# Latent attention: query tiles split into plain and turned parts, unpadded

## Chip, cores and metric

One core of a Trainium2 chip runs the whole program. The metric is the device time of one execution in microseconds; lower is better. The five engines are TensorE (PE, with weight loads shown apart as PEld), VectorE (DVE), ScalarE (ACT), GpSimd (POOL) and SyncE (SP, which issues most of the transfers here).

## What is computed

Three transformer blocks in a row over 256 tokens of width 1024, in float32: a gated mixer with a feed-forward layer, a differential attention with a convolutional feed-forward layer, and a latent attention with a second such layer. The change lies in the latent attention alone. Its 16 heads have a plain query part of 64 values and a turned (rotary) part of 32; the turned part of the keys is one for all heads. Cut to that:

```python
def mla_attention(h, w_in, q_norm_g, kv_norm_g, w_uq, w_ukv, w_o, cos, sin):
    proj = h @ w_in
    c_q = rms_norm(proj[..., :384], q_norm_g)
    c_kv = rms_norm(proj[..., 384:640], kv_norm_g)
    k_pe = apply_rope(proj[..., 640:], cos, sin)
    q = (c_q @ w_uq).reshape(b, s, 16, 64 + 32)
    q_nope, q_pe = q[..., :64], apply_rope(q[..., 64:], cos, sin)
    kv = (c_kv @ w_ukv).reshape(b, s, 16, 64 + 64)
    k_nope, v = kv[..., :64], kv[..., 64:]
    # for each block of 128 queries
    sc = (einsum('bqhd,bkhd->bhqk', q_nope, k_nope)
          + einsum('bqhr,bkr->bhqk', q_pe, k_pe)) * 96 ** -0.5
    p = masked_softmax(sc, mask)
    o = einsum('bhqk,bkhe->bqhe', p, v)
    return o.reshape(b, s, 1024) @ w_o
```

## The kernel before

Activations lie with their features on the partitions and the 256 tokens along the free dimension. Almost every product of a weight is made three times in float32r, from the high and low halves of weight and activation (`mm3`), each of 128x128 weights and 256 columns. A weight comes by a transfer on SP's queue into one of six `raw` buffers (`load_to`), and is split into its halves three parts ahead of its use: ScalarE copies the high half (line 178), VectorE subtracts the low one (line 179).

`mla` (from line 973) records its work as steps. First come the two latent groups and their norms, the keys (`w_k`, in two halves of the heads) and the values (`v_group`). A pair `p` of heads is then treated in five kinds of steps:

- `q_group(p)`, line 1060: one column group of two 128-row tiles, one for each head of the pair, three k-tiles deep, so 18 products. A head's 96 query rows are padded with zeros to 128: plain part, turned part and zeros, in another order for the second head. `q_evac` (line 1064) turns the whole tile by `rope` (lines 852 to 862): a shuffle, two products with tables and a sum on VectorE and GpSimd.
- `scores(p)`, line 1104: for each head, one product for queries 0 with keys 0 and one for queries 1 with all keys, over 128 rows in plain float32 (lines 1110, 1111); then mask, maxima, one small product, exponentials with their sums on ScalarE (line 1121), reciprocal (line 1124) and division (line 1126). The keys lie padded likewise in two arrays, `ke` and `ko`, into which ScalarE copies the plain parts (line 1079) and spreads the turned part (line 1054).
- `trans(p)`, line 1129: three transposes for each head on TensorE (line 1134), a copy by ScalarE.
- `values(p)`, line 1140: eight recorded passes in two column halves of the array.
- `rows`: 24 products of the output weight's part `p`.

From line 1164 on a round `p` = 3 to 9 holds `q_group(p)`, `trans(p - 2)`, `scores(p - 1)`, the output rows of `p - 4` and `values(p - 2)`. Scores, transposes, values and query groups share four PSUM banks (`at_bank`); query tiles, probabilities and their transposes share ten SBUF buffers (tag `t2`).

Steps are recorded in this order, but the framework that makes the program places each engine's instructions in its own fixed order: by the order of the steps, except that an instruction it expects not to be ready is passed by a later one. In the trace output rows stand ahead of transposes, for instance, and scores between two transposes. On the chip each engine then keeps to that order and waits where something isn't there.

The first attention (`diff_attention`, from line 636) has heads of 64 rows; its score products (lines 721, 722) read either half of the partitions.

Of the kernel before, what the change touches and what calls it, by code (L numbers as in the profile page):

```python
# [16 lines left out]
P = 128  # L17
# [34 lines left out]
def _tables():  # L52
# [7 lines left out]
    ml = np.zeros((P, 2, 2, T), np.float32)  # L60
    ml[:, 0] = 1.0
    kp = np.zeros((P, 2, T), np.float32)
    for slot, o in ((0, 64), (1, 32)):
        ml[o:o + 16, 0, slot], ml[o + 16:o + 32, 0, slot] = c16, c16
        ml[o:o + 16, 1, slot], ml[o + 16:o + 32, 1, slot] = -s16, s16
# [3 lines left out]
    return da, ml, kp  # L69


class Unit:
    """A part of a weight on chip: its two float32r halves, made when it is near its use."""
# [11 lines left out]
class Builder:  # L85
# [114 lines left out]
    def cols(self, banks, u, n, kk, stride, xh, xl, first, last, tiles=None):  # L200
        """Adds one k-tile's products to column tiles; two tiles share a bank."""
# [5 lines left out]
    def group(self, units, banks, ncol, xh, xl, nk=KD, between=None, bank=None):  # L207
        """Steps of one column group, k outermost. banks: list filled at the first step."""
# [90 lines left out]
    def mean_sq(self, ss, n):  # L299
        """Mean of squares + EPS by token, [128, 2]."""  # L300
# [16 lines left out]
    def bcast(self, d, tag="rbc"):  # L317
        """r by token along the free dimension, on all partitions: [128, 256]."""
# [15 lines left out]
    def halves(self, src, hi, lo, eng=None):  # L334
        """Exact float32r halves of an SBUF value."""
# [36 lines left out]
        # what is loaded before the raw part of that number  # L372
# [13 lines left out]
    def stats(self, out, n=D, ss=None):  # L386
        """Two steps: the first gives r by token, the second r along the free dimension."""
# [8 lines left out]
    def token_group(self, units, banks, nk, xh, xl, first=None, between=None):  # L396
        """A 512-wide product with tokens on partitions: two banks, one for each token block."""
# [18 lines left out]
    def mixer(self):  # L416
# [9 lines left out]
        # v: tokens on partitions  # L426
# [31 lines left out]
        # u  # L458
# [12 lines left out]
        # spatial gating, two groups at a time  # L471
# [23 lines left out]
        # cg * xs and its convolution  # L495
# [36 lines left out]
        # gates and the two projections, 512 columns at a time  # L532
# [47 lines left out]
    def conv(self, y, z, name, k, n, bias):  # L580
        """Causal convolution of three taps along the free dimension of one tile."""
# [55 lines left out]
    def diff_attention(self):  # L637
# [6 lines left out]
        def one():  # L644
# [15 lines left out]
            # lambda  # L660
# [49 lines left out]
        def scores(n):  # L710
            # one head; columns: queries 0 with keys 0, queries 1 with keys 0 and 1
# [23 lines left out]
            # p0 / sum0 - lam * p1 / sum1 = (p0 - lam * sum0 / sum1 * p1) / sum0  # L735
# [23 lines left out]
        def values(p):  # L759
            # aT columns: queries 0 with keys 0, queries 1 with keys 0, queries 1 with keys 1  # L760
# [15 lines left out]
            # the rows are still to be divided by sum0  # L776
# [197 lines left out]
    def mla(self):  # L974
# [89 lines left out]
        def q_evac(p):  # L1064
            q[p] = self.rope(qb[p][0], self.ml_c, self.ml_s, swap)
# [244 lines left out]
```

## Time and profile before

| | us |
|---|---|
| median of three runs | 1028.51 |
| lowest, highest | 1023.44, 1029.25 |
| profiled execution, first to last instruction | 1028.4 |
| TensorE busy in it | 1004.9 (98%) |
| VectorE busy in it | 747.3 (73%) |
| ScalarE busy in it | 569.6 (55%) |
| GpSimd busy in it | 174.8 (17%) |

The latent attention, up to the last product of its output rows, lies at about 735 to 830 us of the span. A busy time counts durations from an instruction's start to its end; products overlap each other in TensorE, so the distance between starts tells what one costs there. A product in plain float32 is recorded as two passes. "128\*128" or "64\*128" in a row are the rows and columns of the array in use. A bracket at a row's end is the engine's idle time ahead of it and what ended it.

### The profile page before, as it was taken

The numbers are of one execution on the slowest core, as the hardware profiler recorded it, in microseconds if no ns is written. First come the engines' busy times: TensorE is split into PE (matmuls) and PEld (weight loads), VectorE is DVE, ScalarE is ACT, GpSimd is POOL, SyncE is SP. The second block draws the span as 40 slices with busy tenths as digits, with TensorE's granted clock in tenths as the row PEclk, the third lists the DMA queues.
The fourth block names the chain that finished last, engine by engine and source line by source line (L and its number), as shares of the span: only waits on it lengthen the run. The fifth ranks groups of instructions, "written<-read, shape, count | busy, mean of one in ns | idle before, by whom it ended". The sixth has DMA issues, their size and how long they took to land.

```text
span 1028.4 us, 19647 instructions
## 1 busy us (share of the span) xinstructions
PE 1004.9 (98%) x7934; PEld 967.1 (94%) x7934; DVE 747.3 (73%) x1124; ACT 569.6 (55%) x895; POOL 174.8 (17%) x121
## 2 busy tenths in 40 slices
PE   8999999999999999989899999999998999999997
PEld 6999999999999999988799999999997999999995
DVE  5767766567655655778867977777889988877774
ACT  5744454545444444736665765555686667555552
POOL 3001300002311211451202211010421121101001
PEclk9999999999999999999999999999999999999998
DMA  8764555555555555354245465555453435655531
GB/s 322 240 244 170 184 184 185 188 189 171 192 185 185 184 185 188 116 202 134 101 158 185 157 219 178 191 184 156 157 181 126 145 123 192 203 197 186 184 103 41
DMA packets 50923, 180.36 MB, mean 175 GB/s; under 512 B 5648, under 2 KB 5904, under 8 KB 50832
## 3 DMA queue, kind: packets, MB, share of 16 engines
q1 hardware_dynamic: 50544, 178.58, 51.3%
q8 instruction: 62, 1.02, 0.4%
q10 hardware_dynamic: 288, 0.52, 0.1%
q14 instruction: 29, 0.24, 0.1%
HBM read 178.04 MB, written 1.05 MB: 174 GB/s over the span
## 4 chain that ended last, share of the span: by engine, by line
PE 87%; DVE 4%; ACT 3%; POOL 2%; issue 2%; DMA 1%; SPq 0%; POOLq 0%; DVEq 0%; ACTq 0%
PE mm L193 59%; PE at L193 24%; DVE lo L179 1%; DVE t L862 1%; ACT hi L178 1%; POOL tiny L308 1%; POOL xg L689 1%; DMA xg<-in_xg 1%; PE at L1111 1%; PE at L1134 1%; POOL t L861 1%; ACT b L733 0%; ACT t L1121 0%; PE at L481 0%; ACT b L265 0%
## 5 line engine op out<-in xcount | busy, mean ns | idle before, releaser
L193 PE MATMUL mm<-b,hi 128*128 128x256 f32 x3584 | 642.3, 281 | 1.1 <-DVE b L1023 0.8
L193 PEld LDWEIGHTS mm<-b,hi 128*128 128x128 f32 x3584 | 549.3, 188 | 5.0 <-issue 2.1
L179 DVE TENSOR_TENSOR lo<-raw,hi 128x1024 fp32r<-128x1024 f32 (+2 forms) x336 | 415.9, 1250 | 185.5 <-ACT hi L178 184.6
L178 ACT CAST hi<-raw 128x1024 fp32r<-128x1024 f32 (+2 forms) x337 | 345.4, 1036 | 307.7 <-PE mm L193 237.2
L193 PE MATMUL mm<-b,lo 128*128 128x256 f32 x1792 | 501.1, 280 | 0.0
L193 PEld LDWEIGHTS mm<-b,lo 128*128 128x128 f32 x1792 | 336.9, 188 | 0.7 <-issue 0.7
L193 PE MATMUL at<-b,hi 128*128 128x256 f32 x1088 | 194.3, 280 | 1.0 <-POOL b L337 1.0
L193 PEld LDWEIGHTS at<-b,hi 128*128 128x128 f32 x1088 | 166.3, 188 | 2.2 <-POOL b L337 1.2
L193 PE MATMUL at<-b,lo 128*128 128x256 f32 x544 | 152.0, 279 | 0.0
L193 PEld LDWEIGHTS at<-b,lo 128*128 128x128 f32 x544 | 102.0, 188 | 0.0
L886 POOL TENSOR_TENSOR t<-t,t 128x512 f32<-128x512 f32 x22 | 40.4, 1835 | 289.6 <-DVE t L589 251.1
L589 DVE SCALAR_TENSOR_TENSOR t<-t,par,t 128x254 f32<-128x254 f32 (+1 forms) x176 | 76.1, 486 | 11.6 <-ACT t L587 11.0
L280 POOL TENSOR_TENSOR t<-t,t 128x512 f32<-128x512 f32 x18 | 25.5, 1417 | 190.2 <-ACT t L279 189.7
L193 PE MATMUL at<-hi,b 128*128 128x512 f32 x176 | 56.7, 394 | 0.0
L336 ACT CAST b<-t 128x512 fp32r<-128x512 f32 x50 | 30.9, 621 | 42.1 <-POOL t L886 36.2
L331 DVE TENSOR_TENSOR t<-mm,rbc 128x512 f32<-128x512 f32 x76 | 51.6, 687 | 0.2
L193 PE MATMUL mm<-hi,b 128*128 128x512 f32 x144 | 49.7, 418 | 1.4 <-ACT hi L178 1.4
L337 POOL TENSOR_TENSOR b<-t,b 128x512 fp32r<-128x512 f32 x16 | 29.7, 1864 | 124.7 <-ACT b L336 124.7
L587 ACT ACTIVATE t<-t,par 128x256 f32<-128x256 f32 x88 | 46.0, 591 | 6.4 <-DVE t L331 6.4
L337 DVE TENSOR_TENSOR b<-t,b 128x512 fp32r<-128x512 f32 x34 | 24.3, 719 | 22.8 <-ACT b L336 22.8
L193 PEld LDWEIGHTS at<-hi,b 128*128 128x128 f32 x176 | 32.9, 187 | 7.7
L193 PEld LDWEIGHTS mm<-hi,b 128*128 128x128 f32 x144 | 28.5, 199 | 8.5 <-ACT hi L178 2.1
(181 smaller groups left out, 710.0 us busy)
## 6 DMA issues: line engine op xcount, KB each, us to landing
raw<-in_ffn_up SPq DMA_DIRECT2D x88, 512.0 KB, 4.5
raw<-in_w_ff SPq DMA_DIRECT2D x64, 512.0 KB, 3.6
raw<-in_w_in SPq DMA_DIRECT2D x55, 512.0 KB, 4.9
raw<-in_ffn_down SPq DMA_DIRECT2D x44, 512.0 KB, 3.9
raw<-in_da_qk SPq DMA_DIRECT2D x16, 512.0 KB, 4.9
raw<-in_w_proj_a SPq DMA_DIRECT2D x8, 512.0 KB, 4.3
raw<-in_w_proj_b SPq DMA_DIRECT2D x8, 512.0 KB, 4.1
raw<-in_w_out SPq DMA_DIRECT2D x8, 512.0 KB, 4.7
```

The costliest lines, as they stand in the source:

```text
L178: self.nc.scalar.copy(hi[:, sl], w[:, sl])
L179: (u.eng or self.nc.vector).tensor_tensor(lo[:, sl], w[:, sl], hi[:, sl].bitcast(F32), op=ALU.subtract)
L193: self.nc.tensor.matmul(out, lhsT, rhs, start=start, stop=stop, skip_group_check=True)
L280: nc.gpsimd.tensor_tensor(self.ss, self.ss, sq, op=ALU.add)
L308: self.nc.gpsimd.tensor_tensor(r, ms, self.mhalf[:, :n], op=ALU.pow)
L331: self.nc.vector.tensor_tensor(o, bank, self.over2(r), op=ALU.mult)
L336: self.nc.scalar.copy(hi, src)
L337: (eng or self.nc.vector).tensor_tensor(lo, src, hi.bitcast(F32), op=ALU.subtract)
L587: nc.scalar.activation(y, z, AF.Identity, scale=w[2], bias=bias)
L589: nc.vector.scalar_tensor_tensor(out=y[:, d:], in0=z[:, :T - d], scalar=w[2 - d], in1=y[:, d:], op0=ALU.mult, op1=ALU.add)
L689: nc.gpsimd.tensor_tensor(xp, xp, self.over2(st["rx"]), op=ALU.mult)
L886: nc.gpsimd.tensor_tensor(y[0], y[0], y[1], op=ALU.mult)
```

## The change

The padding goes. The 1,536 query columns are ordered into six groups of 256 without zeros: two groups (0 and 3) hold the turned parts of eight heads each, two tiles of four heads, and four groups hold the plain parts of four heads each, two tiles of two heads. Turned groups go through `rope` with the table of the keys, plain groups through one copy on ScalarE; the 512 KB table `ml_tab` and its load go. The plain keys lie in one unpadded array `k`; the turned keys stay where they are computed (`kpe`), without being spread, and GpSimd's two memsets of the padding go.

The scores of a pair become four products over 64 rows (plain part, one head in either half of the partitions) and four over 32 rows (turned part) that add to the same PSUM banks. Both heads' maxima, sums and reciprocals lie in one small tile, so that the product with the scale and the reciprocal are one instruction for both heads. `q_group(1)` moves ahead of the second half of the keys, `scores(1)` ahead of `trans(0)`, and later query groups stand in rounds 3, 4 and 6.

```diff
-        w_uq = self.weights(a["mla_uq"], 1536, 2)
+        w_uq = self.weights(a["mla_uq"], 768, 1)
...
-            bufs["ke"], bufs["ko"] = self.b8(), self.b8()
+            bufs["k"] = self.b8()
             bufs["oh"], bufs["ol"] = self.b8(F32R), self.b8(F32R)
-            nc.gpsimd.memset(bufs["ke"][96:128, :, :], 0.0)
-            nc.gpsimd.memset(bufs["ko"][0:32, :, :], 0.0)
...
-        def k_spread():
-            z = bufs["kpe"]
-            for key, o in (("ke", 64), ("ko", 32)):
-                nc.scalar.copy(bufs[key][o:o + 32, :, :],
-                               z[o:o + 32, :].unsqueeze(1).to_broadcast([32, 8, T]))
...
-        def q_evac(p):
-            q[p] = self.rope(qb[p][0], self.ml_c, self.ml_s, swap)
+        def q_evac(i):
+            if i % 3 == 0:
+                qr[i // 3] = self.rope(qb[i][0], self.kp_tab[:, 0, :], self.kp_tab[:, 1, :], swap)
+            else:
+                j = {1: 0, 2: 1, 4: 2, 5: 3}[i]
+                qn[j] = self.t2()
+                nc.scalar.copy(qn[j], qb[i][0])
...
-                for key, o in (("ke", 0), ("ko", 64)):
-                    nc.scalar.copy(bufs[key][o:o + 64, sl, :], kb[h][i][o:o + 64])
+                nc.scalar.copy(bufs["k"][:, 4 * h + 2 * i:4 * h + 2 * i + 2, :], kb[h][i])
...
         def scores(p):
-            pp[p] = []
+            blocks = ((slice(0, P), slice(0, P)), (slice(P, 384), slice(0, T)))
+            bk = [self.at_bank() for _ in range(2)]
+            ps = [b.rearrange("p a t -> p (a t)") for b in bk]
+            for i, (sl, keys) in enumerate(blocks):
+                for h in range(2):
+                    o = slice(64 * h, 64 * h + 64)
+                    nc.tensor.matmul(ps[h][:, sl], qn[p // 2][o, p % 2, i * P:(i + 1) * P],
+                                     bufs["k"][o, p, keys], start=i == 0, stop=False,
+                                     skip_group_check=True)
+            for i, (sl, keys) in enumerate(blocks):
+                for h in range(2):
+                    o = 64 * h + 32 * (p % 2)
+                    o = slice(o, o + 32)
+                    nc.tensor.matmul(ps[h][:, sl], qr[p // 4][o, p % 4 // 2, i * P:(i + 1) * P],
+                                     bufs["kpe"][o, keys], start=False, stop=True,
+                                     skip_group_check=True, tile_position=(o.start, 0))
+            mx, nm, sm, rs = (self.t([P, 2, 2], t, 4) for t in ("mx2", "nm2", "sm2", "rs2"))
             for h in range(2):
-                k = bufs["ko" if h else "ke"][:, p, :]
...
-                nc.tensor.matmul(ps[:, 0:P], q[p][:, h, 0:P], k[:, 0:P], start=True, stop=True)
-                nc.tensor.matmul(ps[:, P:384], q[p][:, h, P:T], k, start=True, stop=True)
...
+            nc.vector.tensor_tensor(nm, mx, st["qs"].unsqueeze(1).to_broadcast([P, 2, 2]), op=ALU.mult)
...
+            nc.vector.reciprocal(rs, sm)
...
         q_group(2)
-        L(q_evac, 2)
+        L(scores, 1)
         L(trans, 0)
-        L(scores, 1)
         L(values, 0)
         for p in range(3, 10):
-            if p < 8:
-                q_group(p)
-                L(q_evac, p)
+            if p in (3, 4, 6):
+                q_group({3: 3, 4: 4, 6: 5}[p])
             L(trans, p - 2)
```

## Rows read from the trace of the kernel before

**Rows 1.** The page's table of busy time, one line.

```profile
PE 1004.9 (98%) x7934; PEld 967.1 (94%) x7934; DVE 747.3 (73%) x1124; ACT 569.6 (55%) x895; POOL 174.8 (17%) x121
```

**Rows 2.** Busy time by stretch; columns as in the first line.

```profile
core 0: us, PE busy (x) PEld busy (x) DVE busy (x) ACT busy (x) POOL busy (x), PEclk, DMA share, GB/s
735.00:830.00 95.00, 91.27 (x707) 83.26 (x706) 83.31 (x211) 67.43 (x145) 18.46 (x15) 1.00 0.43 144
...
766.00:777.00 11.00, 8.95 (x56) 7.43 (x54) 9.85 (x24) 10.52 (x20) 1.27 (x1) 1.00 0.46 162
...
793.00:816.00 23.00, 23.00 (x188) 20.95 (x186) 22.36 (x65) 15.69 (x39) 4.30 (x3) 1.00 0.42 139
```

**Rows 3.** Groups by line, 735 to 830 us: busy, mean ns; idle before, releasers.

```profile
L861 POOL TENSOR_TENSOR t<-t,b 128x512 f32<-128x512 f32 x8 | 10.8, 1345 | 45.0 <-DVE t L859 37.9 <-DVE rs L1124 7.0
L1134 PE MATMUL at<-ident,t 128*128 128x128 f32 x48 | 10.3, 278 | 2.9 <-DVE t L1126 2.5 <-ACT hi L178 0.4
...
L859 DVE STREAM_SHUFFLE t<-at 128x512 f32<-128x512 f32 x8 | 5.9, 742 | 0.0
...
L862 DVE TENSOR_TENSOR t<-t,t 128x512 f32<-128x512 f32 x8 | 5.4, 680 | 0.8 <-POOL t L861 0.8
L860 DVE TENSOR_TENSOR t<-at,b 128x512 f32<-128x512 f32 x8 | 5.4, 670 | 0.0
```

**Rows 4.** TensorE in order of time, a query group: start, us from there, instruction.

```profile
801.50 0.28 PE L193 MATMUL at<-b,lo 128*128 128x256 f32 x1
801.62 0.40 PE L193 MATMUL at<-b,hi 128*128 128x256 f32 x2
...
802.56 0.28 PE L193 MATMUL at<-b,lo 128*128 128x256 f32 x1
```

**Rows 5.** TensorE in order of time, scores of pair 0.

```profile
766.15 0.39 PE L1110 MATMUL at<-b,t 128*128 128x128 f32 x2
766.37 0.60 PE L1111 MATMUL at<-b,t 128*128 128x256 f32 x2
766.80 0.38 PE L1110 MATMUL at<-b,t 128*128 128x128 f32 x2
```

**Rows 6.** TensorE in order of time, 64-row scores of the first attention.

```profile
495.34 0.50 PE L721 MATMUL at<-t,t 64*128 64x128 f32 x4 [0.92 <-DVE t L862]
...
496.20 0.38 PE L193 MATMUL mm<-b,lo 128*128 128x256 f32 x1
496.51 0.50 PE L721 MATMUL at<-t,t 64*128 64x128 f32 x4
...
513.87 0.50 PE L721 MATMUL at<-t,t 64*128 64x128 f32 x4 [0.79 <-DVE t L862]
...
514.63 0.49 PE L721 MATMUL at<-t,t 64*128 64x128 f32 x4
...
515.49 0.50 PE L193 MATMUL mm<-lo,b 128*128 128x512 f32 x1
```

**Rows 7.** TensorE in order of time, transposes and scores in round 7.

```profile
814.00 0.27 PE L1134 MATMUL at<-ident,t 128*128 128x128 f32 x1
814.11 0.39 PE L1110 MATMUL at<-b,t 128*128 128x128 f32 x2
814.33 0.38 PE L1134 MATMUL at<-ident,t 128*128 128x128 f32 x2
```

**Rows 8.** TensorE in order of time, the transposes it waited for.

```profile
772.85 0.61 PE L1134 MATMUL at<-ident,t 128*128 128x128 f32 x3 [0.31 <-DVE t L1126]
...
775.20 0.30 PE L1134 MATMUL at<-ident,t 128*128 128x128 f32 x1 [1.74 <-DVE t L1126]
...
782.52 0.44 PE L1134 MATMUL at<-ident,t 128*128 128x128 f32 x2 [0.48 <-DVE t L1126]
...
790.89 0.30 PE L1134 MATMUL at<-ident,t 128*128 128x128 f32 x1 [0.37 <-ACT hi L178]
```

**Rows 9.** All engines in order of time, the softmax of pair 6.

```profile
815.70 0.36 DVE L1113 MEMSET at<- 64x128 f32 x2
...
819.28 0.16 DVE L1124 RECIPROCAL rs<-sm 128x2 f32<-128x2 f32 x1
...
820.07 0.27 PE L1134 MATMUL at<-ident,t 128*128 128x128 f32 x1
```

More of the change, by code (lines that the diff above doesn't have):

```diff
@@ L68, in _tables @@
         kp[o:o + 16, 1], kp[o + 16:o + 32, 1] = -s16, s16
-    return da, ml, kp
+    return da, kp
 class Unit:
@@ L986, in mla, with buffers @@
         kvb, cqb = [], []
-        def tables():
-            ml = self.b4([2, 2, T])
-            nc.sync.dma_start(out=ml, in_=a["ml_tab"])
-            self.ml_c, self.ml_s = ml[:, 0], ml[:, 1]
+        def buffers():
             bufs["v"] = self.t([P, 2, D], "b8", 7)
-            bufs["ke"], bufs["ko"] = self.b8(), self.b8()
+            bufs["k"] = self.b8()
             bufs["oh"], bufs["ol"] = self.b8(F32R), self.b8(F32R)
-            nc.gpsimd.memset(bufs["ke"][96:128, :, :], 0.0)
-            nc.gpsimd.memset(bufs["ko"][0:32, :, :], 0.0)
         def squares(key, banks, n):
@@ L1049, in k_rope, with q_group @@
             bufs["kpe"] = z
-        def k_spread():
-            z = bufs["kpe"]
-            for key, o in (("ke", 64), ("ko", 32)):
-                nc.scalar.copy(bufs[key][o:o + 32, :, :],
-                               z[o:o + 32, :].unsqueeze(1).to_broadcast([32, 8, T]))
-        ch, cl = lambda k: bufs["cqh"][:, k, :], lambda k: bufs["cql"][:, k, :]
-        qb, q, pp, pT = {}, {}, {}, {}
-        def q_group(p):
-            qb[p] = []
-            self.group(w_uq[p:p + 1], qb[p], 2, ch, cl, nk=3, bank=self.at_bank)
-        def q_evac(p):
-            q[p] = self.rope(qb[p][0], self.ml_c, self.ml_s, swap)
+        ch, cl = lambda k: bufs["cqh"][:, k, :], lambda k: bufs["cql"][:, k, :]
+        qb, qn, qr, pp, pT = {}, {}, {}, {}, {}
+        def q_group(i):
+            qb[i] = []
+            self.group(w_uq[i:i + 1], qb[i], 2, ch, cl, nk=3, bank=self.at_bank)
+            self.step(lambda: q_evac(i))
+        def q_evac(i):
[5 more added lines that the diff above has]
+                nc.scalar.copy(qn[j], qb[i][0])
         kh, kl = lambda k: bufs["kvh"][:, k, :], lambda k: bufs["kvl"][:, k, :]
@@ L1076, in k_evac @@
             for i in range(2):
-                sl = slice(4 * h + 2 * i, 4 * h + 2 * i + 2)
-                for key, o in (("ke", 0), ("ko", 64)):
-                    nc.scalar.copy(bufs[key][o:o + 64, sl, :], kb[h][i][o:o + 64])
-        self.step(tables)
+                nc.scalar.copy(bufs["k"][:, 4 * h + 2 * i:4 * h + 2 * i + 2, :], kb[h][i])
+        self.step(buffers)
         self.group(w_ckv, kvb, 3, xh, xl)
@@ L1091, in mla @@
         self.step(k_rope)
-        self.step(k_spread)
         q_group(0)
-        self.step(lambda: q_evac(0))
+        q_group(1)
         self.group(w_k[1:2], kb[1], 4, kh, kl, nk=2)
-        q_group(1)
-        self.step(lambda: q_evac(1))
         self.step(lambda: k_evac(1))
@@ new lines, in scores @@
+            for h in range(2):
+                nc.vector.memset(bk[h][0:64, :, 64:128], NEG)
+                for i, (sl, _) in enumerate(blocks):
+                    nc.vector.tensor_reduce(mx[:, h, i:i + 1], ps[h][:, sl], axis=AX.X, op=ALU.max,
+                                            negate=True)
+            nc.vector.tensor_tensor(nm, mx, st["qs"].unsqueeze(1).to_broadcast([P, 2, 2]), op=ALU.mult)
+            pp[p] = [self.t([P, 384], "t2", 10) for _ in range(2)]
+            for h in range(2):
+                for i, (sl, _) in enumerate(blocks):
+                    nc.scalar.activation(pp[p][h][:, sl], ps[h][:, sl], AF.Exp, scale=st["qs"][:, i:i + 1],
+                                         bias=nm[:, h, i:i + 1], accum_out=sm[:, h, i:i + 1])
@@ L1129, in trans @@
+            nc.vector.reciprocal(rs, sm)
+            for h in range(2):
+                for i, (sl, _) in enumerate(blocks):
+                    nc.vector.tensor_scalar(pp[p][h][:, sl], pp[p][h][:, sl], rs[:, h, i:i + 1], None,
+                                            op0=ALU.mult)
         def trans(p):
@@ L1260, in _arrays @@
         z[key] = np.ascontiguousarray(s.transpose(1, 0, 2).reshape(1, P, 2048))
-    uq = i["mla_w_uq_2"][0].reshape(384, 16, 96)
-    pad = np.zeros((384, 8, 2, P), np.float32)
-    pad[:, :, 0, 0:96] = uq[:, 0::2]
-    pad[:, :, 1, 32:64] = uq[:, 1::2, 64:96]
-    pad[:, :, 1, 64:128] = uq[:, 1::2, 0:64]
-    s = _cols(pad.reshape(384, 2048), [r(256 * j, 256 * j + 256) for j in range(8)], 3)
-    z["mla_uq"] = np.ascontiguousarray(s.reshape(4, 2, P, 768).transpose(0, 2, 1, 3).reshape(4, P, 1536))
+    turned = [np.concatenate([r(96 * h + 64, 96 * h + 96) for c in (4 * j, 4 * j + 4) for h in (c, c + 2, c + 1, c + 3)])
+              for j in (0, 2)]
+    plain = [np.concatenate([r(96 * h, 96 * h + 64) for h in range(4 * j, 4 * j + 4)]) for j in range(4)]
+    z["mla_uq"] = _cols(i["mla_w_uq_2"][0], [turned[0], plain[0], plain[1], turned[1], plain[2], plain[3]], 3)
     z["mla_w_o"] = _cols(i["mla_w_o_2"][0], full, 2)
```

27 lines of the change are left out of this document (2 added, 25 removed).

## Prediction

> **What bounds the kernel now.** First the page's table of busy time: TensorE is busy 98% of the span [rows 1]. Such a share says where to look, not what an edit is worth, so the second view is busy time by stretch for the latent attention, 735 to 830 us [rows 2]. TensorE is at work in 91.27 of those 95 us at full granted clock (1.00, 2.4 GHz). From 793 to 816 us it has no idle time at all, with VectorE close behind (22.36 of 23 us); the largest idle part, 2.05 us, lies in 766 to 777 us. So what a product costs TensorE here is paid in full, what another engine saves is paid only where TensorE waits for that engine, and all such waiting comes to 3.7 us. The third view, groups of instructions by line, puts 2.9 us of it ahead of the transposes of the probabilities [rows 3]. The rest of the working is TensorE's order of time, read by the distance from one start to the next, since the durations overlap.
>
> **The change part by part, in TensorE time.**
>
> *Query products.* Eight groups of 18 products become six: 36 products of 128x256 fewer. Nine such products start between 801.50 and 802.56 us [rows 4], 0.118 us each. 36 x 0.118 = **-4.2 us**.
>
> *Scores.* Before, a head is one 128-column and one 256-column product over 128 rows, each recorded as two passes: 0.65 us from one head to the next (766.15 to 766.80), 1.31 us for a pair [rows 5]. After, a pair has eight products: four over 64 rows (heads on partitions 0-63 and 64-127), then four over 32 rows. Products over 64 rows are in the trace of before, in the first attention: there the two halves' passes start almost together, so a block of this very size takes 0.86 us (495.34 to 496.20), not 1.31 [rows 6]. But a block has a price around it: from the full-array product at 496.20 to the next block 0.31 us pass where 0.12 is normal, so 0.19 to enter; and of the 0.86 only 0.65 is array time, 0.21 more. An excursion out of the full array costs 0.40 us beyond its products. Two blocks with no full-array product between them take 0.76 and 0.86 us (513.87, 514.63, 515.49) [rows 6], with the entry 1.81 us; two separate excursions would be 2 x (0.19 + 0.86) = 2.10 us. A pair of heads after is two such blocks, one of 64 and one of 32 rows. No row shows a step from 64 to 32 rows: at least it costs like staying (1.81, 0.50 over before), at most like a full excursion (2.10, 0.79 over). The nearest row is the change between 128 and 64 rows, a change of the same kind but from a fuller array, so I take the middle, 0.65. 8 x 0.65 = **+5.2 us**, bounds +4.0 and +6.3. That the 32-row products run two side by side, as the 64-row ones do, is taken from the same rows; if not, see the rivals.
>
> The Trainium skill, page "TensorEngine Tiling (Array Packing)", section "Key Properties", says that changing the tiling mode, not merely the tile, drains the engine. The 0.19 us entry agrees. By that rule the step from 64 to 32 rows is a full switch, the term would be +6.3 and the sum below 1.1 us higher; the page gives no figure.
>
> *Breaks in the scores.* TensorE's instructions stand in a fixed order that was fitted to expected readiness: in seven pairs the second head's transposes are cut into by the first head's scores (814.00, 814.11, 814.33) [rows 7]. On one array shape that cutting is free. After, each transpose between two score products is one more excursion, 0.40 us. None if the order comes out clean, two in a pair if both heads' transposes cut in; I take one in each of seven pairs, **+2.8 us**, bounds 0 and +5.6.
>
> *Idle ahead of the transposes.* The four waits are 0.31, 1.74, 0.48 and 0.37 us [rows 8]. The first two (pair 0) come because only one token group and one query group stand between scores(0) and trans(0), while VectorE turns a query tile among the softmax's steps. After, scores(1), about 2 us of TensorE, stands ahead of trans(0), and group 2 is a plain tile that ScalarE copies. Both should go, -2.05. The third lies beside the turning of group 3, which stays a turned group: kept. The fourth is released by ScalarE's weight copies, two of which go: I give it up as gone. **-2.4 us**, bounds 0 and -2.9.
>
> *Merged tiny steps.* One reciprocal for both heads waits for the last of four exponentials, and both heads' scores end together. Before, pair 6 goes from the first step on VectorE (815.70) to the first transpose (820.07) in 4.4 us [rows 9], with head 0 being divided before head 1's reciprocal at 819.28. After, head 0's probabilities come when head 1's reciprocal did, about 0.5 us later, 4.9 us in all. Between scores and transposes TensorE has the values (about 0.9 us) and 24 products of the output rows (24 x 0.118 = 2.8), 3.7 us, where no query group falls: 1.2 us short, in four rounds (p = 5, 7, 8, 9). Against that, VectorE loses the turning that used to lie in this chain, and the next pair's scores may move in. Bounds 0 and 4 x 1.2 = +4.8; nearest row: the pairs with no query group before (rounds 8 and 9), where no wait of TensorE shows, so I take a tenth, **+0.5 us**.
>
> *At nothing, with what hides it.* Six turned tiles fewer take from VectorE 6 x (0.74 + 0.67 + 0.68) = 12.5 us and from GpSimd 6 x 1.35 = 8.1 us [rows 3]; 16 tiny steps go; ScalarE loses the spreading of the turned keys and half its key copies, and gains four tile copies; two weight parts fewer are loaded and split; GpSimd's two memsets and the 512 KB table on SP's queue go. TensorE is the one at work meanwhile (100% from 793 us) [rows 2], so this pays nothing beyond the idle already counted. The earlier splits and loads that it permits meet DMA engines that are 0.42 busy in 793-816 us [rows 2]; no stall follows. The tables gone, nothing new queues on SP or GpSimd. One thing gets tighter: query tiles now live for two to four pairs in the pool of ten `t2` buffers. In round 4 I count four of them plus six for probabilities and their transposes, exactly ten; a wait there would delay an exponential by less than the 0.86 us of a block, and I put it at nothing.
>
> **Sum.** -4.2 + 5.2 + 2.8 - 2.4 + 0.5 = **+1.9 us** on the profiled execution, whose span is 1028.4 us and whose surroundings I leave as they are; the median shown is 1028.51, so the two agree within 0.1 us. Forecast **1030.4 us**: no change. The most favourable bounds give -4.2 + 4.0 + 0 - 2.9 + 0 = -3.1, the least +12.5.
>
> **Rivals.**
>
> *B, the clean order:* no breaks, no price for 64 to 32 rows, all waits gone: 1028.5 - 3.1 = **1025.4 us**. For it: the order is fitted anew and VectorE has slack to deliver in time. Against it: transposes cut into scores in nearly every pair of before [rows 7].
>
> *C, the broken scores (slower):* scores have become a filler wherever a transpose waits, and after a transposes-scores-transposes cut every return costs 0.40 us. With four breaks in each of eight pairs, 12.8 in place of 2.8: **1040.4 us**, 1.2% slower. It decides from 3.5 breaks a pair: without breaks the sum is -0.9, and +10.3 takes 28 of them. Against it: a pair has only two heads' transposes, and one cut is what the rows show.
>
> *D, the 32-row products run one after another:* then the second block takes 1.31 of array time, not 0.65: 8 x 0.65 = 5.2 more, **1035.6 us**. Against it, the 64-row blocks [rows 6]; for it, no row has 32-row products.
>
> *E, the softmax comes late:* the 1.2 us of the merged steps show in all four rounds, +4.8 in place of +0.5: **1034.7 us**.
>
> **Chances and range.** A, the forecast with one break a pair, give or take one and the bounds of the switch (own range 1026.5 to 1034): 0.52. B 0.22, C 0.08, D 0.11, E 0.07. The range that leaves out no more than two in ten is 1023 to 1037: it takes in B, D, E and the lower part of C, and below B reaches to the fastest of the three runs of before (1023.44), since their own scatter is 5.8 us. About 1% (10.3 us) is what a measurement of this kernel can tell from no change. Faster by that would need 7 us that no row offers: 0.04. Slower by that is C, or D with E and two breaks: 0.10. Within it: 0.86.
>
> **What would show it right or wrong.** In the changed trace: 108 query products in place of 144; plain score products in two streams whose starts nearly coincide, and the turned ones after them likewise (if spaced like single products, D); from the first plain product of an undisturbed pair to the next full-array product 1.6 to 1.9 us; the count of transposes or other full-array products between two scores of a pair (about one; four would be C); the idle ahead of the transposes under 0.6 us (more than 3 us would be E); VectorE's busy time in the stretch down by about 17 us with the end unmoved. What would make the forecast wrong is a wait that no row shows, above all a transpose that waits for the merged reciprocal, or a step between 64 and 32 rows that costs more than a full excursion.

## The result, and the profile after

The changed kernel takes **1036.53 us** in the median (1032.78 to 1039.58) beside 1028.88 us for the kernel before on the same chip: ratio **1.0085, 95% interval 1.0061 to 1.0110**. It is slower by 8.7 us by the ratio, by 7.7 between these medians. Forecast were 1030.4 us and no change.

Runs of one and the same kernel scatter by up to 10 us here, and the profiles enter the latent attention at different times, so traces are compared by the length of the stage: from the first product that sums the squares of the latent rows (L295 before, L290 after) to the first turning of tokens into rows for the last product (L924 before, L919 after). Before it runs from 745.03 to 851.82, 106.8 us; after from 743.14 to 859.73, 116.6 us. It grew by 9.8 us; the two profiled executions differ by 8.7 (spans 1037.1 and 1028.4), so the loss lies in this stage.

The page after, table of busy time:

```profile
PE 1008.9 (97%) x7962; PEld 964.4 (93%) x7962; DVE 732.1 (71%) x1082; ACT 564.1 (54%) x891; POOL 162.8 (16%) x113
```

Beside [rows 1], VectorE lost 15.2 us of work and GpSimd 12.0, as the change promises. Nothing of it was paid out. Busy time by stretch, after, with columns as in its first line:

```profile
core 0: us, PE busy (x) PEld busy (x) DVE busy (x) ACT busy (x) POOL busy (x), PEclk, DMA share, GB/s
770.00:777.50 7.50, 3.66 (x32) 2.62 (x30) 4.99 (x14) 4.67 (x12) 0.00 (x0) 1.00 0.17 59
777.70:784.40 6.70, 5.07 (x23) 4.35 (x24) 1.61 (x6) 2.33 (x9) 0.00 (x0) 0.50 0.24 88
784.60:794.00 9.40, 9.40 (x73) 7.81 (x72) 6.65 (x18) 5.41 (x14) 1.27 (x1) 1.00 0.17 57
```

TensorE, which [rows 2] showed with almost nothing to wait for, is at work in half of the first stretch, and in the second it works at a granted clock of 0.50, its lower level. TensorE in order of time says what it waits for:

```profile
772.78 0.87 PE L1131 MATMUL at<-ident,t 128*128 128x128 f32 x6
779.33 1.92 PE L188 MATMUL at<-t,b 128*64 128x256 f32 x8 [5.67 <-ACT t L1134]
781.18 0.80 PE L188 MATMUL at<-b,hi 128*128 128x256 f32 x2
...
784.88 0.82 PE L1131 MATMUL at<-ident,t 128*128 128x128 f32 x6
...
826.21 0.76 PE L1131 MATMUL at<-ident,t 128*128 128x128 f32 x4 [0.47 <-DVE t L1123]
...
830.75 1.24 PE L188 MATMUL mm<-b,hi 128*128 128x256 f32 x5 [0.48 <-ACT b L1145]
...
834.41 1.07 PE L1131 MATMUL at<-ident,t 128*128 128x128 f32 x6 [0.19 <-DVE t L1123]
835.64 1.32 PE L188 MATMUL at<-t,b 128*64 128x256 f32 x8 [0.16 <-ACT t L1134]
837.43 0.86 PE L188 MATMUL mm<-b,hi 128*128 128x256 f32 x5 [0.46 <-ACT b L1145]
```

The transposes of pair 0 at 772.78 have no idle time ahead of them any more, where [rows 8] had 0.31 and 1.74 us. But the next step, the values of pair 0, waits 5.67 us for the copies of those transposes. Then the values take 1.85 us from start to start (779.33 to 781.18) and 18 query products 3.70 (781.18 to 784.88), where 0.81 and 2.12 are normal: 2.6 us lost to the clock. From 826 us on, in the rounds without a query group, there are small waits: 1.8 us of idle time by the brackets, about 2.9 us by the distances from start to start.

Why the copies come so late is read from ScalarE and VectorE in order of time (ScalarE first):

```profile
771.96 2.04 ACT L173 CAST hi<-raw 128x1024 fp32r<-128x1024 f32 x2
776.83 0.46 ACT L1118 ACTIVATE t<-at,nm,tiny 128x128 f32<-128x128 f32 x1 [2.83 <-DVE nm L1114]
...
778.80 0.86 ACT L1134 COPY t<-at 128x384 f32<-128x384 f32 x2
...
773.14 0.62 DVE L1112 TENSOR_REDUCE mx<-at 128x1 f32<-128x128 f32 x2
...
773.86 1.20 DVE L174 TENSOR_TENSOR lo<-raw,hi 128x1024 fp32r<-128x1024 f32 x1
774.99 0.60 DVE L1112 TENSOR_REDUCE mx<-at 128x1 f32<-128x128 f32 x2
775.51 1.21 DVE L174 TENSOR_TENSOR lo<-raw,hi 128x1024 fp32r<-128x1024 f32 x1
776.64 0.15 DVE L1114 TENSOR_TENSOR nm<-mx,tiny 128x4 f32<-128x4 f32 x1
```

The transposes were done by 773.7, and ScalarE was idle from 774.0. Yet its next instructions in order are the four exponentials of pair 1, since the change puts scores(1) ahead of trans(0); they wait for the merged maxima (L1114), which VectorE gives at 776.64, behind two weight splits. The copies follow at 778.80. A chain that TensorE does not need yet stands ahead of one that it needs at once.

### The profile page after: what moved, and what is told of

It reads as the page before. It is cut to its first block, busy times and chain, and to the rows that moved or that the text cites. A ratio compares the mean times of both kernels' runs of the same rounds, so it can differ in the third digit from the quotient of the medians.

```text
span 1037.1 us, 19619 instructions
## 1 busy us (share of the span) xinstructions
PE 1008.9 (97%) x7962; PEld 964.4 (93%) x7962; DVE 732.1 (71%) x1082; ACT 564.1 (54%) x891; POOL 162.8 (16%) x113
## 4 chain that ended last, share of the span: by engine, by line
PE 88%; DVE 4%; ACT 3%; issue 2%; POOL 2%; DMA 1%; SPq 0%; POOLq 0%; DVEq 0%; ACTq 0%
PE mm L188 59%; PE at L188 24%; DVE lo L174 1%; PE at L1098 1%; PE at L1105 1%; POOL tiny L303 1%; POOL xg L684 1%; ACT hi L173 1%; DMA xg<-in_xg 1%; DVE t L857 1%; ACT b L260 0%; PE at L1131 0%; ACT b L728 0%; ACT t L1118 0%; POOL t L856 0%
## 5 line engine op out<-in xcount | busy, mean ns | idle before, releaser
L188 PE MATMUL at<-b,hi 128*128 128x256 f32 x1064 | 191.0, 281 | 1.0 <-POOL b L332 1.0
L188 PEld LDWEIGHTS at<-b,hi 128*128 128x128 f32 x1064 | 163.7, 189 | 2.0 <-POOL b L332 1.2
L188 PE MATMUL at<-b,lo 128*128 128x256 f32 x532 | 149.0, 280 | 0.0
```

Source lines behind the costliest of these rows:

```text
L188: self.nc.tensor.matmul(out, lhsT, rhs, start=start, stop=stop, skip_group_check=True)
```

## The experiments

The theory after reading the traces had two parts: *the queue* (ScalarE's copies stand behind the next pair's exponentials) and *the merging* (both heads' probabilities come when the later head's do). The rival to both was *the products*: scores dearer than their term by some switch between array shapes. The expectations call the queue Q, the merging M (or L, the late softmax that comes of it) and the products S. The headings give the names by which they speak of the runs.

**e1, transposes first.** After with two calls exchanged:

```
         q_group(2)
-        L(scores, 1)
         L(trans, 0)
+        L(scores, 1)
```

> The changed kernel with scores(1) put back behind trans(0), the order that the kernel before has; all else stays. Theory Q (queue): in the changed kernel ScalarE's two copies of the transposes of pair 0 stand in its fixed order behind the four exponentials of pair 1, which come 2.8 us late for VectorE's maxima and weight halves; TensorE waits 5.67 us for them ahead of the values of pair 0, and the granted clock then falls to 0.5 for 6.8 us, which stretches the products after it by another 2.6 us. With the old order the copies stand ahead of the exponentials: wait and slow clock go (-8.3), ahead of the transposes of pair 0 about 0.5 us of idle comes back. Span about 1029, time within 0.3% of the kernel before. Rival S (score products): two blocks of 1.90 us a pair and the changes of array shape carry the loss; they are untouched here, so the time stays at 1.007 to 1.010 of the kernel before. Rival M (merged tiny steps): untouched too, likewise 1.007 to 1.010.

Measured: 1038.94 us, ratio 1.0076 (1.0051 to 1.0100). A miss for the queue as the only cause: the 5.67 us wait went, the time did not, and it lies where the rivals had it. TensorE and then VectorE of this kernel, in order of time:

```profile
783.47 0.76 PE L1131 MATMUL at<-ident,t 128*128 128x128 f32 x4 [1.18 <-DVE t L1123]
...
781.46 0.17 DVE L1120 RECIPROCAL rs<-sm 128x4 f32<-128x4 f32 x1
782.44 0.69 DVE L857 TENSOR_TENSOR t<-t,t 128x512 f32<-128x512 f32 x1 [0.81 <-POOL t L856]
783.04 1.00 DVE L1123 TENSOR_SCALAR t<-t,rs 128x128 f32<-128x128 f32 x4
```

Its busy time by stretch, columns as above:

```profile
785.10:791.80 6.70, 6.70 (x32) 4.70 (x33) 3.29 (x10) 2.01 (x7) 0.00 (x0) 0.50 0.47 160
```

The transposes of pair 1 now wait for the divisions, which stand behind a turning step that waits 0.81 us for GpSimd; the clock falls to 0.50 after this 1.18 us wait, and idle times of 0.2 to 0.7 us follow in the later rounds. Moving the call back took the queue's wait away and left the merging bare.

**e2, scores split into products and softmax.** TensorE keeps the order of after; the softmax of pair 1 is issued behind the transposes of pair 0, so that ScalarE's copies come first:

```
-        L(scores, 1)
+        L(products, 1)
         L(trans, 0)
+        L(soft, 1)
         L(values, 0)
```

> The changed kernel with the step scores(p) cut in two, products and softmax; products(1) stay ahead of trans(0), softmax(1) comes behind it. TensorE's order around pair 0 is that of the changed kernel, and only ScalarE's and VectorE's orders differ: the copies of the transposes of pair 0 stand ahead of the exponentials of pair 1. Theory Q: the 5.67 us wait ahead of the values of pair 0 shrinks to under 1.5 us (a copy takes 0.48 us and two follow each other), the clock stays at full, the time comes to within 0.3% of the kernel before or below it. If the wait came of TensorE's order alone (scores(1) ahead of trans(0)), it would stay at 5 us and more and the time at 1.007 to 1.010. Rivals S and M: 1.007 to 1.010 too.

Measured: 1036.36 us, ratio 1.0058 (1.0041 to 1.0074). ScalarE in order of time, then TensorE:

```profile
772.78 2.04 ACT L173 CAST hi<-raw 128x1024 fp32r<-128x1024 f32 x2
774.67 0.91 ACT L1139 COPY t<-at 128x384 f32<-128x384 f32 x2
...
775.25 1.25 PE L188 MATMUL at<-t,b 128*64 128x256 f32 x8 [0.77 <-ACT t L1139]
```

and the stage by stretch, columns as above:

```profile
770.00:850.00 80.00, 75.40 (x588) 62.46 (x587) 53.07 (x129) 50.20 (x120) 6.14 (x5) 1.00 0.27 88
```

and two lines of the view of waits, TensorE from 745 to 850 us (waited for, us in total, times, longest):

```profile
PE at L1136 <- DVE t L1128: 2.0, 5, 0.6
PE mm L188 <- ACT b L1150: 1.4, 3, 0.5
```

The copies now start at 774.67, the wait shrinks from 5.67 to 0.77 us, and the clock stays at 1.00 through the stage. The queue is shown to be what held TensorE there. But only 2.8 us came back (1.0085 to 1.0058, two intervals that overlap; 3.1 us by the stages, 116.6 to 113.5), short of what theory Q forecast: waits of 0.2 to 0.6 us now stand ahead of the transposes in five rounds, and others behind the values.

**e3, the reorder alone, in the kernel before:**

```
-        L(trans, 0)
         L(scores, 1)
+        L(trans, 0)
```

> The kernel before with one part of the change alone: scores(1) ahead of trans(0). Padded tiles, 128-row scores and separate tiny steps stay. Theory Q: ScalarE's copies of pair 0 fall behind the exponentials of pair 1 here too, so a wait of 3 to 6 us stands ahead of the values of pair 0, in place of the 2.05 us ahead of its transposes, and if the wait is as long as in the changed kernel the clock falls as well: 3 to 8 us slower than the kernel before, 1.003 to 1.008. Rivals S and M: nothing of theirs is in it, so the time is that of the kernel before or up to 2 us better, 0.998 to 1.000.

Measured: 1034.46 us, ratio 1.0042 (1.0027 to 1.0058). The view of waits, as above:

```profile
PE at L193 <- ACT t L1137: 4.1, 1, 4.1
PE at L1134 <- DVE t L1126: 1.4, 3, 0.9
```

The one exchanged call makes a 4.1 us wait ahead of the first values in a kernel with the old scores and the old tiny steps, with the clock at 0.50 behind it; ScalarE's copies start at 779.25, right behind the four exponentials of pair 1. The time lies where theory Q put it, and the queue needs neither the new products nor the merged steps.

**e5, filling the wait.** After with query group 3 moved between trans(0) and values(0):

```
         L(trans, 0)
+        q_group(3)
         L(values, 0)
```

> The changed kernel with query group 3 (18 products, 2.1 us) moved from behind values(0) to ahead of it, behind trans(0). ScalarE's order, and with it the late copies, stays. Theory Q with the clock: the values of pair 0 start as late as before, but 2.1 us of the wait are filled, so about 3.6 us of idle are left; if the clock then stays at full the gain is 2.1 + 2.6 = 4.7 us and the time 1.003 to 1.005 of the kernel before; if it still falls, only the 2.1 us are gained, less what the slow stretch costs elsewhere: 1.006 to 1.008. Rivals S and M: no wait is touched that matters to them, 1.007 to 1.010.

Measured: 1037.69 us, ratio 1.0073 (1.0057 to 1.0089). The view of waits, as above:

```profile
PE at L188 <- ACT t L1118: 4.3, 1, 4.3
```

The filler itself waits 4.3 us: it needs a bank of the products' results that the scores of pair 1 hold until those same late exponentials (L1118) have read them. The ratio is inside what was forecast for a clock that falls, but not for the reason given: no part of the wait was filled. The rivals' range holds it too, so the time alone decides nothing. Work put into a wait helps only if it doesn't need what the wait holds.

**e4, the tiny steps per head again, on top of e2:**

```
-            nc.vector.tensor_tensor(nm, mx, st["qs"].unsqueeze(1).to_broadcast([P, 2, 2]), op=ALU.mult)
...
-            nc.vector.reciprocal(rs, sm)
...
+                nc.vector.tensor_tensor(nm[:, h, :], mx[:, h, :], st["qs"], op=ALU.mult)
...
+                nc.vector.reciprocal(rs[:, h, :], sm[:, h, :])
```

> e2_split_scores with the tiny steps of each head apart again (product with the scale, reciprocal, as in the kernel before). e2 showed that the queue on ScalarE is 2 us of the loss and that 1.0058 stays without it: its last rounds, which have no query group, leave TensorE idle 0.64 to 0.75 us ahead of the first transpose and again behind the values. Theory L (late softmax): those rounds are bound by the way from scores to transposes. If the merged reciprocal is a good part of that way, head 0 comes about 0.5 us earlier here in each of the seven rounds: 2 to 3.5 us, time 1.0025 to 1.004. Theory S (score products): VectorE's order is not what the loss is made of; time 1.0055 to 1.0065, a little worse for sixteen more tiny steps.

Measured: 1029.71 us, ratio **1.0009** (0.9980 to 1.0039). The view of waits, TensorE from 745 to 850 us, is this and no more:

```profile
PE mm L188 <- DVE b L1013: 0.7, 1, 0.7
PE at L188 <- ACT t L1138: 0.5, 1, 0.5
```

The waits of the rounds are gone; the stage is 107.4 us long (743.48 to 850.83) against 113.5 in e2 (743.95 to 857.42). The merging is shown: 16 instructions of some 0.17 us fewer on VectorE cost TensorE about 5 us. By the ratios e2 and e4 differ by 5.0 us, with an uncertainty of about 3.5 from the two intervals; the stages differ by 6.1. That is more than theory L forecast (1.0025 to 1.004), though the interval reaches it. What is left of the change, the new products with 108 in place of 144 query products, is worth nothing either way that an interval of 3 us to each side can tell.

**e6, the turned products left out, on top of e2:**

```
-            for i, (sl, keys) in enumerate(blocks):
...
-                    nc.tensor.matmul(ps[h][:, sl], qr[p // 4][o, p % 4 // 2, i * P:(i + 1) * P],
-                                     bufs["kpe"][o, keys], start=False, stop=True,
-                                     skip_group_check=True, tile_position=(o.start, 0))
```

> e2_split_scores with the eight turned (32-row) score products of each pair left out, so the scores lack their turned part; everything else runs. A block of them takes 0.855 us in the trace, 6.8 us in all. Theory S: TensorE bound all along, 6.8 us less plus what a change of array shape costs, 0.999 of the kernel before or less. Theory L: in rounds that wait for the softmax the 0.855 us turn into idle, so of 6.8 us about half shows: 1.002 to 1.003, and the idle ahead of transposes and output rows grows.

Measured: 1029.54 us, ratio 0.9999 (0.9972 to 1.0025), by the ratios 6.1 us less than e2. By the stages it is 6.9 us less (113.5 to 106.6). The products removed took 8 x 0.85 = 6.8 us by the rows of after shown below, so what went is about their array time; since TensorE waits 1.0 us more than in e2 (6.0 against 5.0 us in the view of waits), a hidden cost of about 1 us isn't excluded, one of 5 is. That speaks against the products as the cause. The forecast of theory L, that only half of it would show, was a miss: idle time did not take up the rest. The ratio itself lies between the two forecasts, and its interval reaches both.

**e9, scores a round earlier.** On top of e2, to give the merged softmax a whole round of cover:

```
-            L(trans, p - 2)
-            if p < 9:
-                L(products, p - 1)
-                L(soft, p - 1)
+            if p < 8:
+                L(products, p)
+                L(soft, p)
             if p > 3:
+                L(trans, p - 2)
```

> e2_split_scores with the scores of each pair one round earlier, ahead of the transposes of the pair two before it. The same products, copies and tiny steps; only more TensorE work lies between a pair's scores and its transposes, and no transpose stands between score products any more. Theory L: the idle in the rounds, about 5 us in e2, falls under 1.5 us, and the six breaks of 0.40 us each go: about 6 us less than e2, 0.999 to 1.001 of the kernel before. Theory S: only the breaks go, 2.4 us, so 1.003 to 1.004.

Measured: 1033.27 us, ratio 1.0073 (1.0044 to 1.0103). A miss. The view of waits, TensorE from 745 to 850 us:

```profile
PE at L188 <- ACT t L1139: 6.6, 5, 2.4
PE at L1136 <- DVE t L1128: 1.1, 1, 1.1
```

ScalarE in order of time, one of the five:

```profile
808.66 0.46 ACT L1123 ACTIVATE t<-at,nm,tiny 128x128 f32<-128x128 f32 x1 [3.81 <-DVE nm L1119]
...
810.62 0.86 ACT L1139 COPY t<-at 128x384 f32<-128x384 f32 x2
```

The waits at the transposes shrank to one of 1.1 us, but the queue came back in five rounds: the copies of a pair stand behind the exponentials of a later pair again, and after one of these waits (2.38 us at 811.16) the clock is at 0.50 for about 3 us.

**e8, unpadded query groups, but padded tiles.** The scores, tiny steps and order of before are kept; the plain and turned parts of six query groups are put by ScalarE into zero-filled tiles, so that on TensorE only the 36 query products go:

```
+            bufs["qe"], bufs["qo"] = self.b8(), self.b8()
...
+                for key, r in (("qe", 0), ("qo", 64)):
+                    nc.scalar.copy(bufs[key][r:r + 64, c:c + 2, :], qb[i][0][r:r + 64])
```

> Unpadded query groups as in the changed kernel (six, 108 products), but ScalarE puts plain and turned parts together into padded query tiles whose zeros GpSimd writes once, and the scores are those of the kernel before: two products of 128 rows a head, separate tiny steps, scores(1) behind trans(0). Theory S: 4.2 us of query products saved, nothing paid for scores, so 0.995 to 0.997. Theory L: the two missing query groups were what lay between scores and transposes in rounds 5, 7 and 8; at 5.6 us of TensorE work a round against a way of 4.4 to 5 us through the softmax with 3.6 us of cover, about 1 us a round comes back as idle, and the time is 0.998 to 1.001.

Measured: 1029.34 us, ratio 1.0002 (0.9972 to 1.0031). The view of waits:

```profile
PE at L1138 <- DVE t L1130: 2.8, 3, 2.1
PE mm L188 <- ACT b L260: 1.4, 1, 1.4
```

The 2.1 us wait is that of the transposes of pair 0 (1.74 us in [rows 8]), now with one padded group less ahead of it, and the clock at 0.50 from 766.0 to 769.4 behind it. The 1.4 us are a wait for ScalarE's norm for the following layer; before has none such. All idle time of the stage is 5.6 us (3.7 before), and 3.4 us at half clock cost about 1.7 by estimate: 3.6 of the 4.2 us that the products gained. The stage is 107.8 us long, 1.0 more than before, so a part of what was given back is not accounted for.

**e10, the merging alone, in the kernel before:**

```
-                nc.vector.tensor_tensor(nm, mx, st["qs"], op=ALU.mult)
...
-                nc.vector.reciprocal(rs, sm)
...
+            nc.vector.tensor_tensor(nm, mx, st["qs"].unsqueeze(1).to_broadcast([P, 2, 2]), op=ALU.mult)
...
+            nc.vector.reciprocal(rs, sm)
```

> One part of the change alone: the kernel before with the tiny softmax steps of a pair's two heads merged, and nothing else. Theory that the merging itself costs time (both heads' exponentials wait for the second head's mask and maxima, both heads' divisions for the fourth exponential): the slack between a pair's scores and its transposes runs out in most of the seven rounds, 0.5 to 0.9 us each, so about 1034 us, ratio 1.004 to 1.006, and the trace shows idle ahead of the transposes or behind the values in most rounds. Rival, the term that was forecast (0.5 us, the slack is enough in a kernel with longer rounds): ratio 1.000 to 1.001. Between the two: the merging costs only where the rounds are short, in the three or four rounds of after that have no query group; then this kernel, with a query group in each of its rounds but one, shows next to nothing, and the price belongs to the two edits together.

Measured: 1042.39 us, ratio **1.0133** (1.0116 to 1.0151), worse than any theory's number. The view of waits, TensorE from 760 to 855 us, and TensorE and VectorE in order of time in one round:

```profile
PE at L1135 <- DVE t L1127: 11.3, 8, 3.8
```

```profile
805.31 0.76 PE L1135 MATMUL at<-ident,t 128*128 128x128 f32 x4 [2.10 <-DVE t L1127]
...
803.29 0.16 DVE L1124 RECIPROCAL rs<-sm 128x4 f32<-128x4 f32 x1
804.27 0.69 DVE L862 TENSOR_TENSOR t<-t,t 128x512 f32<-128x512 f32 x1 [0.82 <-POOL t L861]
804.88 1.00 DVE L1127 TENSOR_SCALAR t<-t,rs 128x128 f32<-128x128 f32 x4
```

All eight pairs wait, 11.3 us together, where before waited 2.9 [rows 3]. The late reciprocal falls into the turning of a query tile: the step that waits 0.82 us for GpSimd gets between the reciprocal and the divisions. VectorE's order of time shows the same in five of the eight pairs, with 0.76 to 0.83 us each time. With the clock at 0.50 for 6.8 us behind the first wait the stage is 120.7 us long (743.16 to 863.89), 13.9 more than before. So the longer rounds, which the rival counted on, did not cover the merging; the turning tiles made it dearer.

**e11, after with the tiny steps per head, its order untouched** (the edit of e4 alone):

> After with the tiny steps per head again, its order untouched. Theory of two causes that add: the wait ahead of the first values stays, because the exponentials of pair 1 still stand ahead of ScalarE's copies of the transposes of pair 0 (shorter by one head's mask and maxima at most, 4 to 5.5 us instead of 5.67, with the clock at 0.5 behind it), and the idle time of the late rounds goes: ratio 1.003 to 1.005. Rival, one cause (the merging alone makes the wait so long): the wait falls under 2 us, the clock stays at 1.00 and the ratio is 1.000 to 1.001.

Measured: 1036.33 us, ratio 1.0075 (1.0059 to 1.0092). The view of waits, TensorE from 760 to 855 us, has one line:

```profile
PE at L188 <- ACT t L1133: 4.6, 1, 4.6
```

Every late wait is gone and the queue's stays, as the theory of two causes had it, 4.6 us and the half clock behind it. The time is not what it forecast (1.003 to 1.005): undoing the merging gives 1.0 us by the ratios here (2.9 by the stages, 116.6 to 113.7) and 5.0 (6.1) once the queue is mended. Each difference of ratios is uncertain by 3 us or more, so that the two prices do not add is not shown by the times. A part of the difference is in the trace, where the score products cost more than in after. TensorE in order of time, e11:

```profile
815.32 1.28 PE L1098 MATMUL at<-b,t 64*128 64x128 f32 x8
816.54 0.92 PE L1105 MATMUL at<-kpe,t 32*128 32x128 f32 x8
```

A 64-row block takes 1.22 us here, and another one at 822.03 too, where 0.86 is normal; four pairs are cut (at 785.62, 792.24, 799.02 and 808.58). By the prices of the breaks below that is 4.3 us in place of the 2.35 of after.

**e12 and e13, toward a faster kernel.** e12 gives the padded tiles of e8 the split of e2; e13 gives e8 a filler, query group 4 ahead of the first transposes:

```
+        L(products, 1)
         L(trans, 0)
-        L(scores, 1)
+        L(soft, 1)
```

```
         q_group(2)
+        q_group(4)
         L(trans, 0)
```

> The version of padded tiles put together on the chip from unpadded query groups (e8), with what the kernel with products ahead of the transposes (e2) showed: TensorE gets the score products of a pair ahead of the transposes of the pair before it, VectorE and ScalarE their softmax behind them. Theory (TensorE's waits set the time): the 2.0 us wait ahead of the first transposes and the half clock behind it (3.4 us at 0.5) go, 3 to 4 us off e8: ratio 0.996 to 0.998. Rival, the wait moves one place on as it did each time before (to the copies or to the next transposes): ratio 0.999 to 1.001.

> The kernel of padded tiles put together on the chip (e8), with query group 4 moved from its round to the place ahead of the first transposes, where e8's TensorE stands for 2.1 us and then runs at half clock for 3.4 us. Its 18 products take 2.1 us, and its bank is one that no score holds (in e12 the products put there waited 0.9 us for one). Theory: wait and half clock go and nothing comes in their place, since the round that loses the group has 7 us of other work: ratio to before 0.996 to 0.998. Rival, seen in e9 and e12: the wait moves on, to the transposes of the round that gave its query group away or to the first values, and the ratio stays at 0.999 to 1.001.

Measured: 1030.60 us, ratio 1.0014 (1.0003 to 1.0024), and 1031.94 us, ratio 1.0040 (1.0017 to 1.0063). Both misses. In both the wait moved on, as the rivals had it, and e13 is slower than its rival's number too. In e12 the view of waits has, between 755 and 855 us:

```profile
PE at L1145 <- DVE mx L1126: 1.5, 1, 1.5
...
PE at L1115 <- ACT t L1132: 0.9, 1, 0.9
```

and in e13, between 750 and 850 us:

```profile
PE at L1114 <- ACT b L1070: 2.1, 2, 1.3
PE at L1138 <- DVE t L1130: 1.8, 4, 0.6
```

The clock stayed at 1.00 in this stage in both, but the score products wait for a bank that pair 0's exponentials still read (0.9 us, e12) or for ScalarE's filling of the tiles (2.1 us, e13), and the transposes wait besides. Both also have the 1.4 us wait of e8 at the following layer. No kernel here beats the one before.

## Why the prediction was wrong

The forecast of no change was wrong by one mis-sized term and one term whose stall moved; the rest of the sum held. That 1036.5 us lies inside the stated range, near the numbers of rivals D and E, is chance: D's products and E's sign (over 3 us of idle time ahead of the transposes; 0.7 in after) did not come. What a measurement can tell was also put too wide, at 1%: the interval here is 0.25% to each side.

**Query products, -4.2: held.** 36 products fewer; no wait for a query product shows in the views of e4 or e8.

**Scores, +5.2: held, a little high.** TensorE in order of time, after, an undisturbed pair:

```profile
763.92 0.40 PE L188 MATMUL mm<-hi,b 128*128 128x512 f32 x1
764.24 0.93 PE L1098 MATMUL at<-b,t 64*128 64x128 f32 x8
765.10 0.92 PE L1105 MATMUL at<-kpe,t 32*128 32x128 f32 x8
765.95 0.50 PE L188 MATMUL mm<-hi,b 128*128 128x512 f32 x1
```

The 64-row block takes 0.86 us and the 32-row block 0.85, 1.71 to the next full-array product, in the 1.6 to 1.9 that the prediction asked for. With the 0.19 us of entry of [rows 6] that is 1.90, 0.59 over the 1.31 of [rows 5], 4.7 us for eight pairs. Rival D (32-row products one after another) falls: 0.85 us is what two side by side take.

By the Trainium skill, page "TensorEngine Tiling (Array Packing)", section "Key Properties", a change of the tiling mode drains the engine, so the step from 64 to 32 rows should cost something. The trace agrees, with a small price: the 64-row block takes 0.86 us ahead of the 32-row one and 0.76 ahead of another 64-row block [rows 6]. A pair as two separate excursions would be 2.10; the rows give 1.90, nearer the 1.81 of staying in one shape.

**Breaks, +2.8: held in size, with other parts.** Three pairs are cut (at 786.47 by the pair's own 32-row products, at 810.81 and 826.90 by transposes), not seven, at 1.25, 0.55 and 0.55 us, 2.35 in all. Rival C (28 breaks) falls.

**Idle ahead of the transposes, -2.4: the step that failed first.** The waits of pair 0 went, as said: 772.78 has none. But the step looked at TensorE's order alone. It put scores(1) ahead of trans(0) as a gain of cover and did not ask what the same move puts ahead of the *next* link, ScalarE's copies. Each call issues work on three engines, and the exponentials of pair 1 went ahead of those copies with the scores. Price: 5.67 us and 2.6 us at the lower clock. e3 shows it with the move alone, e2 shows it mended with TensorE's order unchanged.

**Merged tiny steps, +0.5: the mis-sized term.** The mechanism was named (one reciprocal behind four exponentials; rival E's waits in the rounds without a query group, 1.2 us in each), and of its bounds 0 to 4.8 a tenth was taken because the rounds 8 and 9 of before show no wait. That is where the choice failed: no wait shows only that slack is not below zero. It does not say how much there is. Measured: 2.9 us of late waits in after, 5.0 by the ratios and 6.1 by the stages once the stall is mended (e2 against e4), 13.7 where tiles are turned in the same chain (e10, its stretch at half clock included). In after itself 2.9 us lies inside the bounds, but once the stall is mended the upper one is too low as well: it counted the 0.5 us by which head 0 comes later, and not that a later reciprocal can meet another step of VectorE's fixed order, such as the turning that waits for GpSimd (e10). The prediction had named a transpose that waits for the merged reciprocal as the likeliest way to be wrong; it was the smaller of the two causes in after.

**At nothing: held, with its reverse side.** VectorE's 15 us less and GpSimd's 12 us less moved no end. The pool of ten `t2` buffers shows no wait of its own in the views.

**The sum again,** by what was measured: -4.2 + 4.7 + 2.35 - 2.9 (the four waits of [rows 8]) + 5.67 + 2.6 + 2.9 = +11.1, beside 9.8 by the stages. The late waits stand in it by start distances, the other waits by their brackets; with 1.8 for them too the sum is +10.0. Without the queue and the merging the first four terms give -0.05, and e4, which has neither, stands at +0.9 us (ratio 1.0009, 3 us to each side). The arithmetic of the products was right; the order was not.

What stays open: why undoing the merging is worth less when the queue stays, where e4 and e11 give 5.0 and 1.0 us, each uncertain by 3 us or more, and the dearer score products of e11 are about 2 us of it; and what lets the clock fall, below.

## What to carry to other kernels

When a call is moved to fill one engine's wait, write down for every engine that it issues to what it now stands ahead of: here the move removed 2.05 us ahead of transposes and put 5.67 us (4.1 in e3) ahead of the values, which need the copies of these transposes. With the filler's products issued early and its softmax behind the copies 0.77 us of that wait were left (e2).

Merging small instructions of two independent chains makes both wait for the later one. Here their engine had idle time, so it saved nothing, and the consumer had little slack: the 16 instructions saved are some 2.7 us long in all, and saving them cost about 5 us in e2 (against e4) and 13.7 in the kernel before (e10). Size such a merging by how late the first chain's result becomes, and by the next step in the fixed order that it then lands behind.

## What the runs showed of the hardware that was not expected

Idle time alone did not decide the granted clock. It fell to 0.50 in or behind waits of TensorE of 5.67 us (after), 4.6 us (e11), 4.3 us (e5), 4.1 us (e3), 3.8 us (e10, the first), 2.38 us (e9), 2.1 us (e8) and 1.18 us (e1), and it stayed at 1.00 behind the 1.74 us of [rows 8] in before, the 1.5 us of e12 and, in e10, the 2.10 us at 805.31 and the 2.57 us at 816.11. No run here tells these apart. In after the fall added 2.6 us to a wait of 5.67, so a stall cost nearly half as much again as it shows in the view of waits.

The change from products over 64 rows to products over 32 rows, with nothing of the full array between, cost about 0.10 us: blocks start at 764.24, 765.10 and the next product at 765.95, so the first takes 0.86 us, where the first of two 64-row blocks in a row takes 0.76 [rows 6].
